# Mixer of a decoder trunk: all weight subtractions on VectorE, later differential products and merges, output tiles evacuated pair by pair

## The chip, the cores and the metric

The kernel runs on one core of one Trainium2 chip. The metric is the device time of one execution in microseconds (us). The engines are called PE (TensorE: matmuls), DVE (VectorE), ACT (ScalarE), POOL (GpSimd) and SP (SyncE, which issues the loads). Each of them works through its own list of instructions in the order in which the program holds them, and waits for the others by semaphores.

## What is computed

The program is a decoder trunk of two layers on 256 positions of width 1024. A layer is a half-step SwiGLU feed-forward block, a mixer, and a second feed-forward block; each has a normalization in front and a residual add behind it.

```python
for l in range(DEPTH):
    lam_init = 0.8 - 0.6 * math.exp(-0.3 * l)
    x = x + 0.5 * swiglu(rmsnorm(x, ffn1_norm[l]), ffn1_gate[l], ffn1_up[l], ffn1_down[l])
    x = x + mixer(rmsnorm(x, mix_norm[l]), cos, sin, w_in[l], w_out[l],
                  lambda_q1[l], lambda_k1[l], lambda_q2[l], lambda_k2[l],
                  subln_gain[l], dil_gain[l], lam_init)
    x = x + 0.5 * swiglu(rmsnorm(x, ffn2_norm[l]), ffn2_gate[l], ffn2_up[l], ffn2_down[l])
return rmsnorm(x, final_norm)
```

The mixer projects `h @ w_in` (3072 columns) into queries, keys and values of two attention families. The differential family has 4 heads with two score maps each: the weights are `a = softmax(s0) - lam * softmax(s1)` and the output is `a @ v`, normalized per head. The dilated family has 8 heads, whose three window patterns are merged into one mask here. Both outputs, side by side, are multiplied by `w_out`.

## The kernel before

All matmuls run in the 32-bit PE format with an error-compensated split. A weight tile of 128x1024 is loaded raw; ACT rounds it to a high part (`hi`, a CAST at L271, or at L267 for the columns of queries and keys), and a subtraction `raw - hi` gives the low part (`lo`, a TENSOR_TENSOR at the line behind, L272 or L267). The activations are split alike, as `xs` (high and low) at L328 and L333. PE then adds products of high and low parts. One such cast with its subtraction is a **tick**. Eight split tiles can be held ahead; a tick is skipped when none is free.

The feed-forward blocks are long runs of matmuls with ticks in between. The mixer is written as 112 **steps** of PE work. Steps 0 to 95 are the six column chunks of `w_in`, 16 steps each: queries and keys of the dilated family (chunks 0 and 1), of the differential one (2 and 3), then the values of the differential (4, steps 64 to 79) and dilated family (5, steps 80 to 95). A step of chunks 4 and 5 is three matmuls of 512 columns (L300 to L302). Steps 96 to 111 are the output projection: each multiplies four rows of 128 of `w_out` into one of eight output tiles (`wom`). Steps 96 to 99 and 103 to 106 finish output tiles 0 to 3; steps 100 to 102, 107 and 108 to 111 finish tiles 4 to 7.

What else has to be done is hung onto the steps by a table, `PLAN`: behind the matmuls of a step its jobs are issued, in the order of the text. Since every engine keeps the order of issue, the place of a job in the table decides what stands in front of it on its engine. The jobs that the change touches are these:

- `tick` (cast on ACT, subtraction on DVE) and `tick,p` (the same with the subtraction on POOL).
- `score` and `exp`: PE scores (L751), then for every head a masked minimum on DVE (`expos`, L767) and the exponential on ACT (L768), which also sums the denominators.
- `differ,t` for query block t: DVE inverts the denominators (`rd`, L777), scales (`cf`, L779), and combines the two maps of each head in place (four SCALAR_TENSOR_TENSOR on `exdif`, L782).
- `turnp`: PE transposes the weights (`trpdif`, L798) and ACT copies them out (`late`, L800).
- `value,4,t` and `value,5,t`: ACT scales the projected values (`vdif` L737, `vdil` L731). `vdif` of block 1 is written where the weights of block 0 stood, so it waits for the transposes of `turnp,dif,0,0`.
- `avdif` and `avdil` (PE, L806 and L829), `ndif` and `ndil` (normalization on ACT, DVE and POOL; the last operation of `ndif` is `mof` at L816), `merge` (PE transposes `trmdif` and `trmdil` at L844, then the split of the result on ACT and DVE).

The output tiles are evacuated by `chain` in pairs: DVE adds the first half of a tile to `x` (L880), ACT copies the second half (`half_w`, L377), DVE adds that (L882), ACT makes the high part of the next block's activations (L328), DVE the low part (L333), ACT the squares for the next norm (L338, L341). The first matmul of the next feed-forward block (`g_s`) writes into the PSUM buffer of output tile 4, so it waits for that tile's evacuation. Here `chain` is called once for tiles 0 to 3, behind step 106, and once for tiles 4 to 7, behind step 111.

Of the kernel before, what the change touches and what calls it, by code (L numbers as in the profile page):

```python
# [45 lines left out]
def _two_pi_parts():  # L46
# [20 lines left out]
    10: "norm",  # L67
    11: "tick tick",
    13: "tick",
    14: "tick,p",  # L70
    16: "table",
    17: "rope,0,0 rope,0,1",
    19: "tick",
# [2 lines left out]
    26: "tick",  # L76
    28: "tick",
    32: "rope,1,1",
    34: "tick",
    36: "score,dil,1 tick,p exp,dil,1,0 exp,dil,1,2 exp,dil,1,1 exp,dil,1,3",  # L80
    40: "rope,2,0",
    42: "turnp,dil,1,0 turnp,dil,1,1",
    43: "tick",
    46: "score,dil,0 tick,p exp,dil,0,0 exp,dil,0,2 exp,dil,0,1 exp,dil,0,3",
    47: "turnp,dil,1,2 turnp,dil,1,3",
    48: "rope,2,1",
    50: "tick",
# [3 lines left out]
    61: "tick",  # L91
    64: "rope,3,1",
    65: "tick",
    68: "score,dif,1 tick,p exp,dif,1,0 exp,dif,1,1 exp,dif,1,2 exp,dif,1,3",
    72: "value,4,0 differ,1",
    73: "tick",
    75: "score,dif,0 tick,p exp,dif,0,0 exp,dif,0,1 exp,dif,0,2 exp,dif,0,3",
    77: "turnp,dif,1,0",
    78: "differ,0",
    79: "turnp,dif,1,1",  # L100
    82: "value,4,1 tick",
    83: "turnp,dif,0,0",
    85: "avdif,0",
    86: "avdif,1 ndif,0",
    87: "tick ndif,1",
    88: "value,5,0",
    89: "merge,dif,0",
    90: "avdil,0,0 tick",
    92: "avdil,0,1 merge,dif,1",
    93: "ndil,0 tick",  # L110
    95: "value,5,1",
    96: "avdil,1,0 merge,dil,0",
    97: "avdil,1,1 ndil,1",
    98: "tick",
    99: "tick",
    100: "merge,dil,1",
# [2 lines left out]
    103: "tick",  # L119
    105: "tick",  # L120
    107: "tick",
    109: "tick",
}


# [1 line left out]
def trunk_kernel(ctx: ExitStack, tc: tile.TileContext, a: dict, out: bass.AP):  # L127
# [149 lines left out]
    def take(n):  # L277
        while len(split) < state["taken"] + n:
            for f in split_next():
                f()  # L280
        state["taken"] += n
        return split[state["taken"] - n:state["taken"]]

    def free(n):
        state["freed"] += n

    def tick(n, low="v"):

        got = []
        while len(got) < n and len(split) < min(state["freed"] + 8, total):  # L290
            got.append(split_next(low=low))
        return got

    def ticks(n, low="v"):
        for one in tick(n, low):
            for f in one:
                f()
# [64 lines left out]
    def mmw(ps, xs, wh, wl, start, stop, part="both"):  # L362

        def low():
            T.matmul(ps[:, :S], wl, xs[:, 0], start=False, stop=False)  # L365

        def high():
            T.matmul(ps, wh, xs.rearrange("p j s -> p (j s)"), start=start, stop=stop)  # L368
        if part != "both":
            (high if part == "high" else low)()  # L370
            return
        for f in ((high, low) if start else (low, high)):
            f()
# [33 lines left out]
    def chore(n):  # L407
        for _ in range(min(n, len(chores))):
            chores.pop(0)()
# [78 lines left out]
    def back(groups, src, nm, evac, nxt, order=None, beside=None):  # L488


        places = (acc, acc, acc, acc, scb, scb, trb, trb)
        w, accs = {}, {}
        for n, (hf, gi, d) in enumerate(order or [(h, g, d) for h in range(2) for g in range(len(groups)) for d in range(4)]):
            ks, last = groups[gi], gi == len(groups) - 1
            if d == 0:
                w[hf, gi] = take(len(ks) // 2)
            if gi == 0:
                accs[hf, d] = places[hf * 4 + d](f"{nm}{hf}{d}")
            for i, k in enumerate(ks):
                hi, lo = w[hf, gi][i // 2]  # L500
                c0 = (i % 2) * 512 + d * P
                mmw(accs[hf, d], src(k), hi[:, c0:c0 + P], lo[:, c0:c0 + P],
                    gi == 0 and i == 0, last and i == len(ks) - 1)
            if beside:
                beside(n)
            if d < 3:
                continue
            if not beside and not (last and hf):
                ticks(2)
            if last:  # L510
                chain([(hf * 4 + d, accs[hf, d]) for d in range(4)], evac, nxt)
            elif not beside:
                chore(5)
            free(len(ks) // 2)

    def chain(items, evac, nxt):

        prev = []
        for p in range(0, len(items), 2):
            pair = items[p:p + 2]  # L520
            evac(pair)
            for dt in prev:
                nxt.square(dt)
            prev = [dt for dt, _ in pair]
            for dt in prev:
                nxt.high(dt, x[:, dt])
            for dt in prev:
                nxt.low(dt, x[:, dt])
        for dt in prev:
            nxt.square(dt)  # L530

    def down(hs, nx, nm, nxt):
        def evac(pair):
            os = [half_of(ps, f"d{dt}_{nm}") for dt, ps in pair]
            for o, (dt, ps) in zip(os, pair):
                V.tensor_add(o, ps[:, :S], o)
            for o, (dt, ps) in zip(os, pair):
                V.scalar_tensor_tensor(o, o, 0.5, nx.row, op0=ALU.mult, op1=ALU.mult)
            for o, (dt, ps) in zip(os, pair):
                V.tensor_add(x[:, dt], x[:, dt], o)  # L540
        back([range(k, k + n) for k, n in DOWN], lambda k: hs[k], f"dn{nm}", evac, nxt)
# [114 lines left out]
    def mixer(l, nx, cs, consts, nxt):  # L656
# [220 lines left out]
        def evac(pair):  # L877
# [3 lines left out]
            for o, (dt, ps) in zip(os, pair):  # L881
                V.tensor_add(x[:, dt], x[:, dt], o)  # L882
        back((range(4), range(4, 8)), lambda k: mrg["dif" if k < 4 else "dil"][:, k % 4], f"wo{nm}", evac, nxt,
             OUT, lambda i: beside(len(STEPS) + i))

# [88 lines left out]
    for l in range(DEPTH):  # L974
        hs = up(nx, f"f{l}", "late" if l else "first", None if l else x_in, None if l else {2: rope_consts})
        nxt = Normed((2 + l) * KD, f"m{l}")
        down(hs, nx, f"f{l}", nxt)
        nx, nxt = nxt, Normed((4 + l) * KD, f"s{l}")
        mixer(l, nx, cs[0], consts, nxt)
        nx = nxt  # L980
        if l + 1 < DEPTH:
            hs = up(nx, f"s{l}", "late")
            nxt = Normed((l + 1) * KD, f"f{l + 1}")
# [49 lines left out]
```

## Time and profile before

| | us |
|---|---|
| median of three timed runs | 990.19 (990.14 to 990.96) |
| the profiled execution, its own time | 988.68 |
| its span, first to last instruction | 986.8 |
| PE busy in it | 974.4 (99%) |
| DVE busy | 704.2 (71%) |
| ACT busy | 556.9 (56%) |
| POOL busy | 67.9 (7%) |

The profile shows one execution. Times in its views are counted from the span's start. A row of a timeline gives start and duration in us, engine, line, operation, output<-inputs, and a count of merged instructions; in brackets stands the idle time of the engine ahead of it and what ended it. Matmuls overlap in the pipeline, so the pace of PE is read from one start to the next, not from the durations. The mixers lie at about 196 to 309 us (layer 0) and 680 to 793 us (layer 1).

### The profile page before, as it was taken

The numbers are of one execution on the slowest core, as the hardware profiler recorded it, in microseconds if no ns is written. First come the engines' busy times: TensorE is split into PE (matmuls) and PEld (weight loads), VectorE is DVE, ScalarE is ACT, GpSimd is POOL, SyncE is SP. The second block draws the span as 40 slices with busy tenths as digits, with TensorE's granted clock in tenths as the row PEclk, the third lists the DMA queues.
The fourth block names the chain that finished last, engine by engine and source line by source line (L and its number), as shares of the span: only waits on it lengthen the run. The fifth ranks groups of instructions, "written<-read, shape, count | busy, mean of one in ns | idle before, by whom it ended". The sixth has DMA issues, their size and how long they took to land.

```text
span 986.8 us, 15502 instructions
## 1 busy us (share of the span) xinstructions
PE 974.4 (99%) x5995; PEld 859.4 (87%) x5995; DVE 704.2 (71%) x1270; ACT 556.9 (56%) x994; POOL 67.9 (7%) x67
## 2 busy tenths in 40 slices
PE   8999999999999999999999999999999999999997
PEld 7888888899788888888888888889997888888886
DVE  6887788687668887775578777665876778687542
ACT  7765655356657665564357565454456566675432
POOL 0000000020212000000010000001112120000000
PEclk9999999999999999999999999999999999999999
DMA  9975565634435666565646665552652556656531
GB/s 293 274 217 173 181 198 178 210 129 141 159 100 168 213 214 192 172 204 202 214 140 193 186 206 194 194 211 90 210 169 88 172 161 185 203 177 184 200 129 44
DMA packets 134346, 176.80 MB, mean 179 GB/s; under 512 B 4944, under 2 KB 97280, under 8 KB 134272
## 3 DMA queue, kind: packets, MB, share of 16 engines
q1 hardware_dynamic: 134096, 175.54, 55.5%
q8 instruction: 47, 0.77, 0.3%
q10 hardware_dynamic: 176, 0.27, 0.1%
q14 instruction: 27, 0.22, 0.1%
HBM read 174.75 MB, written 1.05 MB: 178 GB/s over the span
## 4 chain that ended last, share of the span: by engine, by line
PE 93%; DVE 4%; ACT 1%; issue 1%; DMA 1%; SPq 0%; POOLq 0%; POOL 0%; ACTq 0%
PE g_s L368 8%; PE u_s L368 8%; PE dnf L368 8%; PE g_f L368 8%; PE u_f L368 8%; PE u_s L365 4%; PE u_f L365 4%; PE g_f L365 4%; PE g_s L365 4%; PE dnf L365 4%; PE dns L368 4%; PE pj_m L688 3%; PE pj_m L690 3%; PE pj_m L689 3%; PE dns L365 2%; PE dn_last L302 2%
## 5 line engine op out<-in xcount | busy, mean ns | idle before, releaser
L272 DVE TENSOR_TENSOR lo<-raw,hi 128x1024 fp32r<-128x1024 f32 (+1 forms) x293 | 352.8, 1223 | 138.9 <-ACT hi L271 138.1
L271 ACT CAST hi<-raw 128x1024 fp32r<-128x1024 f32 (+1 forms) x297 | 303.4, 1046 | 121.1 <-PE u_f L368 26.0
L368 PE MATMUL g_s<-xs_s,hi 128*128 128x512 f32 x352 | 127.3, 395 | 0.9 <-DVE x L880 0.9
L368 PE MATMUL u_s<-xs_s,hi 128*128 128x512 f32 x352 | 127.3, 395 | 0.0
L365 PE MATMUL u_s<-xs_s,lo 128*128 128x256 f32 x352 | 91.7, 281 | 0.0
L365 PE MATMUL g_s<-xs_s,lo 128*128 128x256 f32 x352 | 91.5, 280 | 0.0
L368 PEld LDWEIGHTS g_s<-xs_s,hi 128*128 128x128 f32 x352 | 66.0, 187 | 12.6 <-DVE x L880 1.5
L368 PEld LDWEIGHTS u_s<-xs_s,hi 128*128 128x128 f32 x352 | 66.0, 187 | 11.1
L688 PE MATMUL pj_m<-xs_m,hi 128*128 128x256 f32 x256 | 73.2, 286 | 0.0
L690 PE MATMUL pj_m<-xs_m,lo 128*128 128x256 f32 x256 | 71.8, 281 | 1.1 <-DVE lo L267 1.1
L689 PE MATMUL pj_m<-xs_m,hi 128*128 128x256 f32 x256 | 71.7, 280 | 0.0
L365 PEld LDWEIGHTS u_s<-xs_s,lo 128*128 128x128 f32 x352 | 66.5, 189 | 3.9
L365 PEld LDWEIGHTS g_s<-xs_s,lo 128*128 128x128 f32 x352 | 66.5, 189 | 3.7
L368 PE MATMUL g_f<-xs_in,hi 128*128 128x512 f32 x176 | 65.1, 401 | 0.0
L368 PE MATMUL u_f<-xs_in,hi 128*128 128x512 f32 x176 | 64.8, 400 | 0.0
L368 PE MATMUL u_f<-xs_f,hi 128*128 128x512 f32 x176 | 63.7, 395 | 0.0
L368 PE MATMUL g_f<-xs_f,hi 128*128 128x512 f32 x176 | 63.5, 394 | 0.0
L690 PEld LDWEIGHTS pj_m<-xs_m,lo 128*128 128x128 f32 x256 | 48.2, 188 | 1.3 <-DVE lo L267 1.3
L688 PEld LDWEIGHTS pj_m<-xs_m,hi 128*128 128x128 f32 x256 | 48.2, 188 | 1.0 <-issue 0.7
L689 PEld LDWEIGHTS pj_m<-xs_m,hi 128*128 128x128 f32 x256 | 48.2, 188 | 0.1
L267 DVE TENSOR_TENSOR lo<-raw,hi 128x1024 fp32r<-128x1024 f32 x28 | 36.0, 1320 | 14.6 <-ACT hi L267 14.6
L267 ACT CAST hi<-raw 128x1024 fp32r<-128x1024 f32 x32 | 31.6, 1048 | 25.6 <-DMA raw<-in_w_in_dram 8.9
(363 smaller groups left out, 2226.1 us busy)
## 6 DMA issues: line engine op xcount, KB each, us to landing
raw<-in_ffn_gate_dram SPq DMA_DIRECT2D x86, 512.0 KB, 4.0
raw<-in_ffn_up_dram SPq DMA_DIRECT2D x86, 512.0 KB, 5.1
raw<-in_ffn_down_dram SPq DMA_DIRECT2D x41, 1024.0 KB, 5.1
raw<-in_w_in_dram SPq DMA_DIRECT2D x24, 1024.0 KB, 5.2
raw<-in_w_out_dram SPq DMA_DIRECT2D x8, 1024.0 KB, 5.0
raw<-in_ffn_down_dram SPq DMA_DIRECT2D x6, 512.0 KB, 3.6
xt<-in_x_dram SPq DMA_DIRECT2D x3, 256.0 KB, 5.3
raw<-in_ffn_gate_dram SPq DMA_DIRECT2D x3, 256.0 KB, 5.5
```

The lines of the kernel that those rows point to most:

```text
L267: out = [lambda: A.copy(hi, raw), lambda: ENGINE[low].tensor_sub(lo, raw, hi.bitcast(F32))]
L271: out.append(lambda sl=sl: A.copy(hi[:, sl], raw[:, sl]))
L272: out.append(lambda sl=sl: ENGINE[low].tensor_sub(lo[:, sl], raw[:, sl], hi[:, sl].bitcast(F32)))
L302: T.matmul(ps, xl, wh, start=False, stop=stop)
L365: T.matmul(ps[:, :S], wl, xs[:, 0], start=False, stop=False)
L368: T.matmul(ps, wh, xs.rearrange("p j s -> p (j s)"), start=start, stop=stop)
L688: T.matmul(ps, hi, nx.xs[k][:, 0], start=k == 0, stop=False)
L689: T.matmul(ps, hi, nx.xs[k][:, 1], start=False, stop=False)
L690: T.matmul(ps, lo, nx.xs[k][:, 0], start=False, stop=k == KD - 1)
```

## The change

The table loses all `tick,p`; plain `tick` entries come at neighbouring steps. `avdif` goes from steps 85 and 86 to 86 and 87, the differential merges from 89 and 92 to 91 and 93, and the dilated products and norms move by up to four steps. In the last part `chain` is called for two tiles at a time, as soon as the second of them is finished: behind steps 104, 106, 109 and 111.

```diff
-    14: "tick,p",
...
-    34: "tick",
-    36: "score,dil,1 tick,p exp,dil,1,0 exp,dil,1,2 exp,dil,1,1 exp,dil,1,3",
+    33: "tick",
+    35: "tick",
+    36: "score,dil,1 exp,dil,1,0 exp,dil,1,2 exp,dil,1,1 exp,dil,1,3",
...
-    46: "score,dil,0 tick,p exp,dil,0,0 exp,dil,0,2 exp,dil,0,1 exp,dil,0,3",
+    45: "tick",
+    46: "score,dil,0 exp,dil,0,0 exp,dil,0,2 exp,dil,0,1 exp,dil,0,3",
...
-    68: "score,dif,1 tick,p exp,dif,1,0 exp,dif,1,1 exp,dif,1,2 exp,dif,1,3",
+    68: "score,dif,1 exp,dif,1,0 exp,dif,1,1 exp,dif,1,2 exp,dif,1,3",
+    70: "tick",
     72: "value,4,0 differ,1",
     73: "tick",
-    75: "score,dif,0 tick,p exp,dif,0,0 exp,dif,0,1 exp,dif,0,2 exp,dif,0,3",
+    75: "score,dif,0 exp,dif,0,0 exp,dif,0,1 exp,dif,0,2 exp,dif,0,3",
+    76: "tick",
     77: "turnp,dif,1,0",
     78: "differ,0",
     79: "turnp,dif,1,1",
-    82: "value,4,1 tick",
+    80: "value,4,1",
     83: "turnp,dif,0,0",
-    85: "avdif,0",
-    86: "avdif,1 ndif,0",
-    87: "tick ndif,1",
-    88: "value,5,0",
-    89: "merge,dif,0",
-    90: "avdil,0,0 tick",
-    92: "avdil,0,1 merge,dif,1",
-    93: "ndil,0 tick",
-    95: "value,5,1",
-    96: "avdil,1,0 merge,dil,0",
-    97: "avdil,1,1 ndil,1",
+    84: "tick",
+    86: "avdif,0",
+    87: "avdif,1 ndif,0",
+    88: "value,5,0 ndif,1",
+    89: "tick",
+    91: "merge,dif,0",
+    92: "tick",
+    93: "merge,dif,1",
+    94: "avdil,0,0 tick",
+    95: "value,5,1 avdil,0,1 ndil,0",
+    96: "avdil,1,0",
+    97: "avdil,1,1 ndil,1 merge,dil,0",
...
-    109: "tick",
+    108: "tick",
...
             if beside:
                 beside(n)
+            if beside and last and d % 2:
+                chain([(hf * 4 + e, accs[hf, e]) for e in (d - 1, d)], evac, nxt)
             if d < 3:
                 continue
-            if not beside and not (last and hf):
-                ticks(2)
-            if last:
-                chain([(hf * 4 + d, accs[hf, d]) for d in range(4)], evac, nxt)
-            elif not beside:
-                chore(5)
+            if not beside:
+                if not (last and hf):
+                    ticks(2)
+                if last:
+                    chain([(hf * 4 + e, accs[hf, e]) for e in range(4)], evac, nxt)
+                else:
+                    chore(5)
             free(len(ks) // 2)
```

What the tables make of it is seen in the order of the built programs. Line numbers of the changed kernel are 4 higher below the table and 7 higher below `back` (L271 is L275, L768 is L775). The order of loads on SP is the same in both. POOL has eight rows less, its four subtractions in each layer; the entry at step 14 issued nothing before, as no tile was free there.

On ACT, around the two blocks of differential exponentials of layer 0, there stood before (`hi` casts, exponentials of block 1 on 256 keys and of block 0 on 128 keys, copies of transposed weights and values):

```order
L271 CAST hi_2822<-raw_2787 128x1024
L768 ACTIVATE exdif_m_2826,den_m_2827<-exdif_m_2826,mxdif_m_2828 128x256 x2
...
L768 ACTIVATE exdif_m_2826,den_m_2827<-exdif_m_2826,mxdif_m_2843 128x256 x2
L737 ACTIVATE late_m_2861<-pj_m_2776,rs_m_2207 128x512
L271 CAST hi_2878<-raw_2876 128x1024
L271 CAST hi_2908<-raw_2876 128x1024
L768 ACTIVATE exdif_m_2912,den_m_2913<-exdif_m_2912,mxdif_m_2914 128x128 x2
...
L768 ACTIVATE exdif_m_2912,den_m_2913<-exdif_m_2912,mxdif_m_2929 128x128 x2
L800 COPY late_m_2861<-trpdif_m_2940 128x512
L800 COPY late_m_2861<-trpdif_m_2962 128x512
L737 ACTIVATE vdif_m_2978<-pj_m_2857,rs_m_2207 128x512
L271 CAST hi_2982<-raw_2980 128x1024
L800 COPY late_m_2861<-trpdif_m_2989 128x512
```

At the same place on ACT there stands now:

```order
L775 ACTIVATE exdif_m_2822,den_m_2823<-exdif_m_2822,mxdif_m_2839 128x256 x2
L275 CAST hi_2850<-raw_2787 128x1024
L744 ACTIVATE late_m_2861<-pj_m_2776,rs_m_2207 128x512
L275 CAST hi_2878<-raw_2876 128x1024
L775 ACTIVATE exdif_m_2908,den_m_2909<-exdif_m_2908,mxdif_m_2910 128x128 x2
...
L775 ACTIVATE exdif_m_2908,den_m_2909<-exdif_m_2908,mxdif_m_2925 128x128 x2
L275 CAST hi_2933<-raw_2876 128x1024
L807 COPY late_m_2861<-trpdif_m_2940 128x512
L807 COPY late_m_2861<-trpdif_m_2962 128x512
L744 ACTIVATE vdif_m_2972<-pj_m_2857,rs_m_2207 128x512
L807 COPY late_m_2861<-trpdif_m_2983 128x512
L275 CAST hi_2994<-raw_2992 128x1024
```

Each of the two casts has moved from ahead of a block of exponentials to behind it, and the cast between `vdif` and the last copy has moved behind that copy.

On DVE, from the last minimum of block 1 to the combination of block 0, there stood before (`lo` is a subtraction, `rd`, `cf`, `exdif`, `de` are `differ`):

```order
L767 ISA mxdif_m_2843 128x1
L777 RECIPROCAL rd_m_2863<-den_m_2827 128x4
L779 SCALAR_TENSOR_TENSOR cf_m_2865<-den_m_2827,lamn,rd_m_2863 128x4
L782 SCALAR_TENSOR_TENSOR exdif_m_2826<-exdif_m_2826,cf_m_2865 128x256 x4
L785 SCALAR_TENSOR_TENSOR de_m_2871<-den_m_2827 128x4
L272 TENSOR_TENSOR lo_2879<-raw_2876,hi_2878 128x1024
L767 ISA exdif_m_2912,mxdif_m_2914<-scdif_m_2888,mask_dif 128x128
...
L767 ISA mxdif_m_2929 128x1
L777 RECIPROCAL rd_m_2949<-den_m_2913 128x4
```

At the same place on DVE there stands now:

```order
L774 ISA mxdif_m_2839 128x1
L276 TENSOR_TENSOR lo_2851<-raw_2787,hi_2850 128x1024
L784 RECIPROCAL rd_m_2863<-den_m_2823 128x4
L786 SCALAR_TENSOR_TENSOR cf_m_2865<-den_m_2823,lamn,rd_m_2863 128x4
L789 SCALAR_TENSOR_TENSOR exdif_m_2822<-exdif_m_2822,cf_m_2865 128x256 x4
L792 SCALAR_TENSOR_TENSOR de_m_2871<-den_m_2823 128x4
L276 TENSOR_TENSOR lo_2879<-raw_2876,hi_2878 128x1024
L774 ISA exdif_m_2908,mxdif_m_2910<-scdif_m_2888,mask_dif 128x128
...
L774 ISA mxdif_m_2925 128x1
L276 TENSOR_TENSOR lo_2934<-raw_2876,hi_2933 128x1024
L784 RECIPROCAL rd_m_2949<-den_m_2909 128x4
```

A subtraction stands now between the minima of each block and its `rd`, where nothing stood.

On DVE, at the evacuation of output tiles 0 to 5, there stood before (`x<-wom` and `x<-x,half_w` are the two adds, `xs_s` the low parts):

```order
L272 TENSOR_TENSOR lo_3261<-raw_3257,hi_3260 128x1024
L272 TENSOR_TENSOR lo_3281<-raw_3257,hi_3280 128x1024
L880 TENSOR_TENSOR x<-wom_3119,x 128x256
...
L333 SCALAR_TENSOR_TENSOR xs_s_3302<-x,gains,xs_s_3302 128x256
L880 TENSOR_TENSOR x<-wom_3177,x 128x256
...
L333 SCALAR_TENSOR_TENSOR xs_s_3321<-x,gains,xs_s_3321 128x256
L272 TENSOR_TENSOR lo_3344<-raw_3340,hi_3343 128x1024
L272 TENSOR_TENSOR lo_3364<-raw_3340,hi_3363 128x1024
L880 TENSOR_TENSOR x<-wom_3205,x 128x256
```

At the same place on DVE there stands now:

```order
L276 TENSOR_TENSOR lo_3261<-raw_3257,hi_3260 128x1024
L887 TENSOR_TENSOR x<-wom_3119,x 128x256
...
L337 SCALAR_TENSOR_TENSOR xs_s_3282<-x,gains,xs_s_3282 128x256
L276 TENSOR_TENSOR lo_3300<-raw_3257,hi_3299 128x1024
L887 TENSOR_TENSOR x<-wom_3177,x 128x256
...
L337 SCALAR_TENSOR_TENSOR xs_s_3321<-x,gains,xs_s_3321 128x256
L276 TENSOR_TENSOR lo_3344<-raw_3340,hi_3343 128x1024
L276 TENSOR_TENSOR lo_3356<-raw_3340,hi_3355 128x1024
L887 TENSOR_TENSOR x<-wom_3205,x 128x256
```

The subtraction of step 105 has moved from ahead of the first pair to between the pairs; on ACT its cast now stands behind the squares of the first pair, and the copies of the second pair behind that cast.

## Rows read from the trace of the kernel before

**Rows 1.** The page, first part: busy time of PE, its share of the span and its instructions.

```profile
PE 974.4 (99%) x5995; PEld 859.4 (87%) x5995; DVE 704.2 (71%) x1270; ACT 556.9 (56%) x994; POOL 67.9 (7%) x67
```

**Rows 2.** Waits of PE in the stretch of the mixer of layer 0, 200 to 330 us (engine, output, line, what it waited for: us in total, times, longest).

```profile
PE pj_m L690 <- DVE lo L267: 1.1, 1, 1.1
PE avf_m L806 <- ACT late_m L800: 0.8, 1, 0.8
PE g_s L368 <- DVE x L880: 0.4, 1, 0.4
```

**Rows 3.** The same view for the mixer of layer 1, 684 to 790 us, and behind it the row of PE's timeline at the end of that mixer.

```profile
PE avf_m L806 <- ACT late_m L800: 0.9, 1, 0.9
...
792.87 0.51 PE L368 MATMUL g_s<-xs_s,hi 128*128 128x512 f32 x1 [0.45 <-DVE x L880]
```

**Rows 4.** Timeline of layer 0 around steps 33 to 36: DVE, POOL and PE.

```profile
217.16 4.56 DVE L267 TENSOR_TENSOR lo<-raw,hi 128x1024 fp32r<-128x1024 f32 x2
...
218.24 2.39 POOL L267 TENSOR_TENSOR lo<-raw,hi 128x1024 fp32r<-128x1024 f32 x1 [13.37 <-ACT hi L267]
...
220.42 0.28 PE L689 MATMUL pj_m<-xs_m,hi 128*128 128x256 f32 x1
221.77 0.39 PE L690 MATMUL pj_m<-xs_m,lo 128*128 128x256 f32 x1 [1.07 <-DVE lo L267]
```

**Rows 5.** Timeline of DVE in layer 0, the two `differ` and what lies between them.

```profile
258.42 0.18 DVE L777 RECIPROCAL rd_m<-den_m 128x4 f32<-128x4 f32 x1 [1.77 <-ACT exdif_m L768]
...
260.56 1.23 DVE L272 TENSOR_TENSOR lo<-raw,hi 128x1024 fp32r<-128x1024 f32 x1
261.69 0.29 DVE L767 CUSTOM_DVE_ANT_0 exdif_m<-scdif_m,mask_dif 128x128 f32<-128x128 f32 x1
...
265.31 0.18 DVE L777 RECIPROCAL rd_m<-den_m 128x4 f32<-128x4 f32 x1 [1.84 <-ACT exdif_m L768]
...
265.79 1.14 DVE L782 SCALAR_TENSOR_TENSOR exdif_m<-exdif_m,cf_m 128x128 f32<-128x128 f32 x4
```

**Rows 6.** Timeline of ACT in the same stretch: casts of steps 73 and 75, `vdif`, and the copy of the last transposes.

```profile
258.87 1.99 ACT L271 CAST hi<-raw 128x1024 fp32r<-128x1024 f32 x2
...
267.40 0.69 ACT L737 ACTIVATE vdif_m<-pj_m,rs_m 128x512 f32<-128x512 f32 x1 [1.17 <-PE trpdif_m L798]
...
268.93 0.59 ACT L800 COPY late_m<-trpdif_m 128x512 f32<-128x512 f32 x1
```

**Rows 7.** Timeline of PE in the same stretch: first and last transposes of the differential weights, matmuls of steps 84 and 85, `avdif,0`.

```profile
261.44 0.60 PE L798 MATMUL trpdif_m<-ident,exdif_m 128*128 128x128 f32 x4
...
266.50 0.80 PE L798 MATMUL trpdif_m<-ident,exdif_m 128*128 128x128 f32 x4
267.06 0.48 PE L300 MATMUL pj_m<-hi,xs_m 128*128 128x512 f32 x1
...
268.32 0.40 PE L302 MATMUL pj_m<-hi,xs_m 128*128 128x512 f32 x1
269.57 1.16 PE L806 MATMUL avf_m<-late_m 128*128 128x128 f32 x8 [0.84 <-ACT late_m L800]
```

**Rows 8.** Timeline of DVE in layer 0, the last operation of `ndif,0` and of `ndif,1`.

```profile
273.39 0.69 DVE L816 TENSOR_TENSOR mof_m<-avf_m,rsf_m 128x512 f32<-128x512 f32 x1 [1.12 <-POOL rsf_m L815]
...
277.14 0.69 DVE L816 TENSOR_TENSOR mof_m<-avf_m,rsf_m 128x512 f32<-128x512 f32 x1 [1.13 <-POOL rsf_m L815]
```

**Rows 9.** Timeline of layer 0 at the end of the output projection: PE (first matmul of step 105, last of step 111, first of the next block), DVE (first adds of pair 0, the subtractions of steps 107 and 109, first adds of the pair of tiles 4 and 5), ACT (high parts of pair 0, squares of the second pair, casts of steps 107 and 109).

```profile
298.96 0.28 PE L365 MATMUL wom<-mgdil_m,lo 128*128 128x256 f32 x1
...
308.45 0.40 PE L368 MATMUL wom<-mgdil_m,hi 128*128 128x512 f32 x1
309.29 0.50 PE L368 MATMUL g_s<-xs_s,hi 128*128 128x512 f32 x1 [0.44 <-DVE x L880]
...
299.70 0.75 DVE L880 TENSOR_TENSOR x<-wom,x 128x256 f32<-128x256 f32 x2
...
306.27 2.63 DVE L272 TENSOR_TENSOR lo<-raw,hi 128x1024 fp32r<-128x1024 f32 x2 [1.07 <-ACT hi L271]
308.82 0.74 DVE L880 TENSOR_TENSOR x<-wom,x 128x256 f32<-128x256 f32 x2
...
300.82 0.91 ACT L328 ACTIVATE xs_s<-x,gains 128x256 fp32r<-128x256 f32 x2 [1.29 <-DVE x L882]
...
304.58 0.71 ACT L341 ACTIVATE sq_s<-x 128x256 f32<-128x256 f32 x2
305.20 1.99 ACT L271 CAST hi<-raw 128x1024 fp32r<-128x1024 f32 x2
```

**Rows 10.** Timeline of PE in the kernel's first microseconds and its last matmul, and the view by windows for the last 2.8 us (columns: busy us and counts of PE, PEld, DVE, ACT, POOL, then granted TensorE clock, DMA share, GB/s).

```profile
5.41 0.77 PE L368 MATMUL g_f<-xs_in,hi 128*128 128x512 f32 x1
...
8.28 0.63 PE L368 MATMUL g_f<-xs_in,hi 128*128 128x512 f32 x1
8.71 0.63 PE L368 MATMUL u_f<-xs_in,hi 128*128 128x512 f32 x1
...
11.02 0.48 PE L365 MATMUL g_f<-xs_in,lo 128*128 128x256 f32 x2
...
980.32 0.28 PE L302 MATMUL dn_last<-hi,hE_s 128*128 128x256 f32 x1
...
984.00:986.80 2.80, 0.00 (x0) 0.00 (x0) 0.00 (x0) 0.00 (x0) 0.00 (x0) 0.50 0.49 182
```

## The prediction

> **What bounds the kernel now.** I read the busy times first: PE is busy for 974.4 of 986.8 us [rows 1], so a change on DVE, ACT or POOL can only show where PE waits for it. Next come the waits of PE in the two stretches that the change touches. In layer 0 there are three: 1.1 us for a subtraction, 0.8 us for a copy of transposed weights in front of `avf`, and 0.4 us for the evacuation add in front of `g_s` [rows 2]. Layer 1 has the last two only [rows 3]. That is all the change can win. What it can lose has to be read from the lists of DVE and ACT: wherever a moved cast or subtraction stands ahead of something that PE needs soon. Steps of chunks 4 and 5 follow each other at 0.234 us a matmul, 0.70 us a step (267.06 to 268.32 is five matmuls and a small start-up) [rows 7]. Times below are those of layer 0; layer 1 has the same lists.
>
> **Term A, subtractions off POOL: 1.2 us won, in layer 0 only.** While POOL's subtraction runs from 218.24 for 2.39 us, two DVE subtractions take 4.56 us together [rows 4]; two others without POOL's beside them take 2.63 us [rows 9] and a single one moves the next instruction on by 1.13 us (260.56 to 261.69) [rows 5]. So DVE lost about 2 us there, and PE stood from 220.42 to 221.77 instead of 0.12 us: 1.23 us. Without the POOL row the second subtraction ends near 219.5, a microsecond before PE wants it. The wait goes. In layer 1 no such wait is listed [rows 3], so nothing is won. The replacements cost DVE 1.13 us each. Those of steps 33, 35 and 45 stand ahead of the dilated minima, where DVE waits for PE's scores or has just got its 2 us back: I cost them at nothing; uncovered, each would be at most 1.13 us.
>
> **Term B, subtractions in front of `differ`: 4.2 us lost per layer.** Here the cover is missing. Before, the inversion of block 1 starts at 258.42, released by the last exponential, after 1.77 us of idle DVE; that of block 0 at 265.31, after 1.84 us [rows 5]. That idle time looks like room for a subtraction of 1.13 us. But its cast now stands on ACT behind all the exponentials of the block. So after the last exponential come a cast (1.99 us for two, so 0.95 to 1.04 for one) [rows 6], then the subtraction (1.13), and only then the inversion: 2.1 us later than before. This happens twice in a row, and the two add up, because the minima of block 0 stand on DVE behind the `differ` of block 1. Inversion 1 moves from 258.42 to 260.5, the minima of block 0 from 261.69 to 263.8, its exponentials with them, and inversion 0 from 265.31 to 269.5. The combination at 265.79 moves to 270.0.
>
> PE is not that patient. The first transposes (261.44) have some room: inversion and two combinations end near 261.9, which costs 0.3 to 0.4 us. The last ones (266.50) have none: already before, four transposes took 0.56 us up to the next matmul (267.06), where other transposes of four take 0.35, since each waits for its head's combination [rows 7]. So PE reaches the matmul at 267.06 as much later as the combinations: 4.2 us, the first wait included. It will stand some 3.5 us in one piece.
>
> **Term C, the copy before `avdif,0`: 1.0 us won per layer.** Before, `vdif` starts at 267.40, after the transposes, then comes a cast, then the copy at 268.93 [rows 6]; `avf` starts at 269.57, though PE could have at 268.32 + 0.23 = 268.55 [rows 7]. Now the copy stands right behind `vdif` and `avdif,0` a step later. With the transposes ending near 271.26, `vdif` starts 0.34 us later and the copy is done 0.69 + 0.59 us after that, at 272.9; PE arrives after three steps, at 273.4. The wait of 1.02 us is gone, with half a microsecond to spare. Terms B and C leave 3.2 us per layer.
>
> **Moved merges and dilated products: nothing.** The last operation of `ndif,0` ended 4.5 us after the start of `avf` (269.57 to 274.08) [rows 7, 8], so now near 277.9; the merge stands behind step 91, which PE reaches near 279.7 (0.9 us for `avdif,0`, 1.7 for `avdif,1`, five steps). `ndif,1` ends near 280.6 with the second merge at 281.6: about 1 us of room. What PE does in this stretch is the same work in another order. If a cover fails, what is late is at most some tenths; I keep 0.5 us per layer for the upper end.
>
> **Term D, evacuation pair by pair: 1.1 us lost per layer.** PE has done output tile 1 at 298.96, yet DVE begins with pair 0 at 299.70, since four subtractions stand ahead of it [rows 9]. Now three do, so the second add of the pair can start as soon as tile 1 can be read, near 299.2. That is the gain meant. Then the pair runs through: from the second add (300.03 before) the high parts come 0.8 us later, and with two squares of 0.71 us together behind them ACT is through 2.35 us after that add, near 301.5. But the cast of step 105 now stands here (to 302.5), its subtraction waits for it (to 303.7), and the second pair starts behind the subtraction. Its squares end 2.7 us later, near 306.4. Behind them stand the casts of two ticks, which began at 305.20 before; `g_s` came 4.09 us after that, at 309.29. So `g_s` comes near 310.4. PE is through its last matmul at 308.45 + 0.23 = 308.68: a wait of 0.6 us becomes 1.7. Adds and copies that were far apart are not faster for being split; a cast on ACT, with its subtraction, is now inside the chain that sets the end. The bounds are 0.6 us won (the wait vanishes) and 1.6 us lost.
>
> **Sum.** Per layer 4.2 - 1.0 + 1.1 = 4.3 us lost; twice that, less 1.2 in layer 0, is 7.3 us. The profiled execution took 988.68 us (span 986.8 and 1.9 around it), which makes 996.0. The median of the timed runs lies 1.5 us above it, so 990.19 + 7.3 = **997.5 us**. The measurement tells 0.2%, 2.0 us, from no change.
>
> **Rivals.** (1) *The tail gains.* Terms A to C hold, but tile 4 is free in time, since the split lets the first pair go early and ACT's squares overlap. Then both waits of 0.6 us go instead of growing: 990.19 + 2 x (3.2 - 0.6) - 1.2 = 994.2. Against it stands the place of the cast and subtraction between the pairs. (2) *The clock falls.* In the last 2.8 us of the kernel the granted clock was 0.50, the level of 1.2 GHz, with PE's last matmul started at 980.32 [rows 10]; so some microseconds without work lower it, and term B makes a gap of 3.5 us where none was above 1.3. At the low level 512 columns take 0.43 us (8.28 to 8.71) [rows 10] instead of 0.234, so each slow microsecond costs half of itself. At the start such a stretch lasted at most from 5.41 to 11.02 [rows 10], so 0 to 2.8 us per gap, 1.4 in the middle: 997.5 + 2.8 = 1000.3. The Trainium skill, "TensorE: Matmul & The Clock Gate", section "Why this matters for your kernels", warns of gaps between bursts of matmuls for this reason: they send the clock back to the half level. By that rule the change would land at this rival's time; no wait within the trace of before is long enough to show it. (3) *Faster.* If the casts reach ACT early enough for the subtractions to fall wholly into the idle 1.77 and 1.84 us ahead of the inversions, term B is nothing, and A, C and the vanished waits of the tail remain: 990.19 - 1.2 - 2 x 1.0 - 2 x 0.6 = 985.8. It decides at a cast that ends 1.13 us before the last exponential; the order on ACT puts it a microsecond behind it. (4) *Nothing to tell:* the gaps of term B are made good by shorter waits later. There are hardly any later waits to shorten [rows 2, 3]. That the change doesn't do what it says is excluded by the order: POOL has no subtraction left.
>
> **How the numbers follow.** Forecast 0.55 (997.5), tail gains 0.13 (994.2), clock falls 0.22 (1000.3), faster 0.07 (985.8), nothing to tell 0.03. The range takes in the first three: from 994.2 less half a microsecond of rounding, 993.7, to the forecast with term D at 1.6, failing covers of 0.5 per layer and most of a clock loss: 997.5 + 1.0 + 1.0 + 2.0 = 1001.5. That leaves out the two last cases and a long slow stretch, under 2 in 10. Slower by over 0.2%: 0.90; within: 0.03; faster: 0.07.
>
> **What would show it.** Right: a new PE wait for DVE `exdif` at the last differential transposes, over 3 us in each layer; the inversions idle only until a subtraction that itself waits for ACT's cast; no PE wait for `late` and none for a projection's `lo`; a wait of 1 to 2 us in front of `g_s`. The granted clock there says whether rival 2 holds. Wrong: no wait at those transposes, which would mean that the cast ran ahead of the exponentials; or `g_s` without a wait, which is rival 1.

## The result: 1001.9 us instead of 990.6, and the profile after

| | before | after |
|---|---|---|
| median of four timed runs, us | 990.58 (990.14 to 991.08) | 1001.91 (1001.0 to 1002.88) |
| profiled execution, own time | 988.68 | 1002.53 |
| its span | 986.8 | 1000.7 |
| mean granted clock of PE | 0.998 | 0.990 |

The changed kernel is slower by 11.3 us: the ratio is 1.0117, 95% interval 1.0105 to 1.013. The time lies 0.4 us above the upper end of the forecast range; the kernel before, timed anew, came out 0.4 us above the 990.19 from which the forecast started.

The page's first row, as in [rows 1]:

```profile
PE 980.8 (98%) x5995; PEld 864.7 (86%) x5995; DVE 705.5 (71%) x1278; ACT 556.3 (56%) x994; POOL 45.7 (5%) x59
```

PE has the same 5995 instructions and is busy 6.4 us longer. While it waits it is not busy, so some matmuls must have run more slowly. The waits of PE over the whole span (columns as in [rows 2]) show the rest:

```profile
PE trpdif_m L805 <- DVE exdif_m L789: 6.9, 2, 3.4
PE g_s L372 <- DVE x L887: 3.6, 2, 1.8
```

The waits of [rows 2, 3] for `lo` and `late` are gone. The one ahead of `g_s` has grown from 0.4 to 1.8 us in each layer, and there is a new one of 3.4 us at the last differential transposes. Their cause stands on DVE, timeline of layer 0, the same stretch as [rows 5]:

```profile
258.08 1.23 DVE L276 TENSOR_TENSOR lo<-raw,hi 128x1024 fp32r<-128x1024 f32 x1 [2.70 <-ACT hi L275]
259.22 0.17 DVE L784 RECIPROCAL rd_m<-den_m 128x4 f32<-128x4 f32 x1
...
262.49 0.28 DVE L774 CUSTOM_DVE_ANT_0 exdif_m<-scdif_m,mask_dif 128x128 f32<-128x128 f32 x1
...
267.04 1.23 DVE L276 TENSOR_TENSOR lo<-raw,hi 128x1024 fp32r<-128x1024 f32 x1 [2.78 <-ACT hi L275]
268.18 0.17 DVE L784 RECIPROCAL rd_m<-den_m 128x4 f32<-128x4 f32 x1
...
268.64 1.14 DVE L789 SCALAR_TENSOR_TENSOR exdif_m<-exdif_m,cf_m 128x128 f32<-128x128 f32 x4
```

The brackets show it: DVE stands for 2.70 and 2.78 us ahead of the two subtractions, last of all for their casts on ACT, and the inversion starts the moment the subtraction is through. PE in the same stretch, as in [rows 7]:

```profile
265.31 0.40 PE L306 MATMUL pj_m<-hi,xs_m 128*128 128x512 f32 x1
269.14 1.02 PE L805 MATMUL trpdif_m<-ident,exdif_m 128*128 128x128 f32 x4 [3.44 <-DVE exdif_m L789]
269.92 0.47 PE L304 MATMUL pj_m<-hi,xs_m 128*128 128x512 f32 x1
...
271.02 0.63 PE L304 MATMUL pj_m<-hi,xs_m 128*128 128x512 f32 x1
271.45 0.63 PE L305 MATMUL pj_m<-lo,xs_m 128*128 128x512 f32 x1
...
273.58 1.12 PE L813 MATMUL avf_m<-late_m 128*128 128x128 f32 x8
```

The reader should look at the starts behind the wait: 271.02 to 271.45 is 0.43 us a matmul of 512 columns, where it was 0.234. The windows over the two gaps of layer 0 (columns as in [rows 10], the third from the end is the granted clock):

```profile
269.00:270.00 1.00, 0.86 (x5) 0.58 (x5) 0.85 (x4) 0.00 (x0) 0.00 (x0) 1.00 0.54 31
270.00:271.00 1.00, 1.00 (x4) 0.80 (x4) 0.00 (x0) 0.74 (x2) 0.00 (x0) 0.65 0.88 340
271.00:272.00 1.00, 1.00 (x4) 0.78 (x3) 0.00 (x0) 1.00 (x2) 0.00 (x0) 0.50 1.04 406
272.00:273.00 1.00, 1.00 (x4) 0.81 (x3) 0.59 (x1) 0.37 (x1) 0.00 (x0) 0.50 0.71 272
273.00:274.00 1.00, 1.00 (x6) 0.81 (x6) 0.63 (x1) 0.00 (x0) 0.00 (x0) 0.64 0.00 0
274.00:275.00 1.00, 1.00 (x9) 0.92 (x8) 0.00 (x0) 0.26 (x1) 0.00 (x0) 1.00 0.00 0
...
314.00:315.00 1.00, 1.00 (x6) 0.88 (x7) 0.87 (x3) 0.43 (x2) 0.00 (x0) 0.84 0.57 33
315.00:316.00 1.00, 1.00 (x4) 0.85 (x4) 0.88 (x2) 1.00 (x5) 0.07 (x1) 0.50 0.68 190
...
317.00:318.00 1.00, 1.00 (x5) 0.81 (x5) 1.00 (x3) 0.22 (x1) 0.46 (x1) 0.50 1.08 375
318.00:319.00 1.00, 1.00 (x7) 0.91 (x6) 0.76 (x3) 1.00 (x4) 0.00 (x0) 0.96 0.23 72
```

After both gaps PE resumes at full clock, and about a microsecond later the clock is granted at 0.50 (1.2 GHz) for about three microseconds. In layer 1 the same happens behind `g_s`. Behind its transposes, where PE resumes at 759.90, the clock has fallen while PE still stood, and it is back at 765.2 only:

```profile
758.00:759.00 1.00, 0.00 (x0) 0.00 (x0) 1.00 (x2) 0.73 (x2) 0.00 (x0) 0.70 0.00 0
759.00:760.00 1.00, 0.10 (x1) 0.13 (x1) 0.93 (x6) 0.00 (x0) 0.00 (x0) 0.50 0.00 0
...
764.00:765.00 1.00, 1.00 (x5) 0.81 (x4) 0.54 (x1) 0.00 (x0) 0.00 (x0) 0.50 0.00 0
765.00:766.00 1.00, 1.00 (x9) 1.00 (x9) 0.00 (x0) 0.00 (x0) 0.00 (x0) 0.88 0.00 0
```

The end of the output projection, as in [rows 9]: PE, then DVE, and below it the adds of the second pair before the change.

```profile
311.74 0.40 PE L372 MATMUL wom<-mgdil_m,hi 128*128 128x512 f32 x1
313.93 0.50 PE L372 MATMUL g_s<-xs_s,hi 128*128 128x512 f32 x1 [1.80 <-DVE x L887]
```

```profile
306.14 1.23 DVE L276 TENSOR_TENSOR lo<-raw,hi 128x1024 fp32r<-128x1024 f32 x1 [1.08 <-ACT hi L275]
307.28 0.75 DVE L887 TENSOR_TENSOR x<-wom,x 128x256 f32<-128x256 f32 x2
...
310.89 2.65 DVE L276 TENSOR_TENSOR lo<-raw,hi 128x1024 fp32r<-128x1024 f32 x2 [1.06 <-ACT hi L275]
313.46 0.74 DVE L887 TENSOR_TENSOR x<-wom,x 128x256 f32<-128x256 f32 x2
```

```profile
302.17 0.75 DVE L880 TENSOR_TENSOR x<-wom,x 128x256 f32<-128x256 f32 x2
```

The subtraction between the pairs waits 1.08 us for its cast and moves the next instruction on by 1.14. The adds of the second pair start 5.1 us later than before (302.17, now 307.28), and those of tiles 4 and 5 4.6 us later (308.82 [rows 9], now 313.46), where PE's last matmul is 3.3 us later.

**Where the 13.9 us between the two spans lie**, read from the shift of the same matmul in both traces. Start of the last `pj` ahead of the first differential transposes: 261.21, now 259.93, -1.28. `pj` behind the last transposes: [rows 7] 267.06, now 269.92, +2.86. `avf`: 269.57 plus the step that it was moved by (0.70), now 273.58, +3.31. Last matmul of step 111: [rows 9] 308.45, now 311.74, +3.29. `g_s`: 309.29, now 313.93, +4.64. Behind the slow stretch there (`ssp_s`, 316.38, now 322.56): +6.18. Layer 1 repeats it: last `pj` ahead of the first transposes 744.81, now 750.70, +5.89; behind the last transposes 750.68, now 760.73, +10.05; `avf` 753.18 plus 0.70, now 764.72, +10.84; last matmul of step 111 792.03, now 803.05, +11.02; `g_s` 792.87 [rows 3], now 805.23, +12.36; `ssp_s` 799.97, now 813.88, +13.91.

### The profile page after: what moved, and what is told of

Read it like the earlier page. It is cut to its first block, busy times and chain, and to the rows that moved or that the text cites. A ratio compares the mean times of both kernels' runs of the same rounds, so it can differ in the third digit from the quotient of the medians.

```text
span 1000.7 us, 15499 instructions
## 1 busy us (share of the span) xinstructions
PE 980.8 (98%) x5995; PEld 864.7 (86%) x5995; DVE 705.5 (71%) x1278; ACT 556.3 (56%) x994; POOL 45.7 (5%) x59
## 4 chain that ended last, share of the span: by engine, by line
PE 92%; ACT 3%; DVE 3%; issue 1%; DMA 0%; SPq 0%; POOLq 0%; POOL 0%; ACTq 0%
PE g_s L372 8%; PE u_s L372 8%; PE u_f L372 8%; PE g_f L372 8%; PE dnf L372 8%; PE u_s L369 4%; PE g_s L369 4%; PE u_f L369 4%; PE g_f L369 4%; PE dnf L369 4%; PE dns L372 4%; PE pj_m L695 3%; PE pj_m L697 3%; PE pj_m L696 3%; PE dns L369 2%; PE dn_last L306 2%
## 5 line engine op out<-in xcount | busy, mean ns | idle before, releaser
L276 DVE TENSOR_TENSOR lo<-raw,hi 128x1024 fp32r<-128x1024 f32 (+1 forms) x297 | 357.6, 1222 | 152.9 <-ACT hi L275 149.8
L275 ACT CAST hi<-raw 128x1024 fp32r<-128x1024 f32 (+1 forms) x297 | 303.9, 1046 | 121.0 <-PE u_f L372 25.8
L372 PEld LDWEIGHTS u_s<-xs_s,hi 128*128 128x128 f32 x352 | 67.1, 191 | 11.3
L271 DVE TENSOR_TENSOR lo<-raw,hi 128x1024 fp32r<-128x1024 f32 x32 | 38.3, 1236 | 14.6 <-ACT hi L271 14.6
L369 PE MATMUL u_f<-xs_f,lo 128*128 128x256 f32 x176 | 45.8, 281 | 0.0
```

The lines of the kernel that those rows point to most:

```text
L271: out = [lambda: A.copy(hi, raw), lambda: ENGINE[low].tensor_sub(lo, raw, hi.bitcast(F32))]
L275: out.append(lambda sl=sl: A.copy(hi[:, sl], raw[:, sl]))
L276: out.append(lambda sl=sl: ENGINE[low].tensor_sub(lo[:, sl], raw[:, sl], hi[:, sl].bitcast(F32)))
```

## Experiments

Each kernel was timed next to the kernel before. Its median there was 990.6 for both subtractions moved, for four tiles at once (with and without them moved) and for the pairs alone; 989.8 for the fillers and for the parts in the kernel before; 990.0 for the rest. Ratios and the distances that are compared are to that median: the changed kernel stands 11.3 us above its own.

**Both subtractions out of the way.** The ticks in front of the inversions are issued earlier and later:

```diff
     65: "tick",
+    67: "tick",
...
-    70: "tick",
...
-    76: "tick",
     77: "turnp,dif,1,0",
-    78: "differ,0",
+    78: "differ,0 tick",
```

> The changed kernel with its tick of step 70 at step 67 (cast and subtraction ahead of the exponentials of block 1) and its tick of step 76 at step 78, behind differ,0. Theory (the loss comes from a cast and a subtraction standing in front of each inversion, and from the clock falling behind the gap): PE's wait at the last differential transposes goes from 3.4 us to under 0.4 in both layers, the granted clock stays at 1.00 there, the wait at g_s stays near 1.8; the time falls from 1001.9 to about 992.6 (990 to 994). Rival (load: VectorE simply has four more subtractions per layer and PE waits for it wherever they stand): the wait only changes its place, the time stays above 999.

Measured: 989.95 us (989.43 to 992.12), ratio 0.9995 (0.9986 to 1.0005). No wait at the transposes is left, so VectorE's load is not what PE waits for. The time is 2.6 us under the one expected, just below its range. It stands 0.7 us below the kernel before, so these two entries cost 12.0 us. Of that 2 x 4.1 is lost ahead of the transposes; the other 3.8 is what is left for the clock behind the two waits. The next two move one of them at a time (one half of the diff each).

> Changed kernel with only the cast and subtraction of step 70 issued at step 67, ahead of the exponentials of block 1; the subtraction in front of the inversion of block 0 stays. Theory (each of the two subtractions puts 2.1 us into the wait at the last transposes, and they add up): that wait becomes 1.2 to 1.5 us instead of 3.4 in both layers, and the time falls by 2 x 2.0 to 997.9 as far as the work goes. What the clock does behind a gap of that length is open: if it stays, as in the kernel before, where the longest gap was 1.07 us, another 2 x 1.6 go and the time is 994.5; if it falls, 997.9. Rival (they overlap, the later one alone makes the wait): the wait stays over 3 us and the time within 1 us of 1001.9.

> Changed kernel with only the cast and subtraction of step 76 issued behind the combination of block 0; the subtraction in front of the inversion of block 1 stays. Theory: the same 2.1 us go from the wait at the last transposes, which becomes 1.2 to 1.5 us; the wait at the first transposes (some tenths) stays. Time 994.5 if the clock stays up behind such a gap, 997.9 if it falls. The two kernels of this pair should lie within 1.5 us of each other. Rival (the first subtraction is hidden by idle DVE time and costs nothing): this kernel lies at 990, like the one with both moved, and its sister at 1001.

Measured: 995.95 us (994.89 to 997.97) and 993.68 us (991.52 to 995.17). PE of the first, the last transposes in layers 0 and 1, and below it the second, layer 0:

```profile
267.50 1.03 PE L805 MATMUL trpdif_m<-ident,exdif_m 128*128 128x128 f32 x4 [1.68 <-DVE exdif_m L789]
...
756.23 1.02 PE L805 MATMUL trpdif_m<-ident,exdif_m 128*128 128x128 f32 x4 [1.68 <-DVE exdif_m L789]
```

```profile
267.54 1.02 PE L804 MATMUL trpdif_m<-ident,exdif_m 128*128 128x128 f32 x4 [1.37 <-DVE exdif_m L788]
```

Neither is hidden: moving one takes 1.8 or 2.1 us off the wait of 3.4, moving both all of it. Both rivals fall. The two lie 2.3 us apart, further than forecast. The waits differ by 2 x 0.3 us; the clock may account for the rest, since in the profiled executions it fell behind three of the first kernel's four gaps and one of the second's.

**Four tiles at once again** (the rest as changed; the tick of step 108 goes back to 109):

```diff
-            if beside and last and d % 2:
-                chain([(hf * 4 + e, accs[hf, e]) for e in (d - 1, d)], evac, nxt)
...
+            if last:
+                chain([(hf * 4 + d, accs[hf, d]) for d in range(4)], evac, nxt)
```

> The changed kernel with the evacuation of four tiles at once and the last tick at step 109, as before the change. Theory (the tick between the two pairs is what makes g_s late, and its gap lowers the clock too): the wait at g_s falls from 1.8 to about 0.4 us, the clock stays at 1.00 behind it, the wait at the transposes stays at 3.4; the time falls from 1001.9 to about 998.5 (997 to 999.5). Rival (the pairwise evacuation wins, as the split is meant to; the g_s wait comes from the stretch being later as a whole): no change or slower, 1001.5 to 1003.

Measured: 996.89 us (996.66 to 997.87), ratio 1.0065 (1.005 to 1.008), 6.3 above the kernel before, so 5.0 less than the changed kernel. Its waits of PE:

```profile
PE trpdif_m L802 <- DVE exdif_m L786: 6.9, 2, 3.4
...
PE g_s L372 <- DVE x L884: 0.9, 2, 0.4
```

The clock stays at 1.00 behind `g_s` and falls behind the transposes only. Of the 5.0 us, 2 x 1.35 is waiting, which leaves 2.3 for the clock. The reverse puts the pairs alone into the kernel before.

> The kernel before with the pairwise evacuation alone, and its last tick at step 108. Theory: g_s waits about 1.8 us in each layer instead of 0.4, and the clock falls behind it; 990.6 + 2 x 1.35 + 0 to 3.1 is 993.3 to 996.4. Rival (splitting wins once the stretch is not late): the wait at g_s goes, 989.4.

Measured: 995.69 us (994.98 to 995.9), ratio 1.005 (1.0035 to 1.0065). The wait ahead of `g_s` is 1.8 us in both layers, and the clock fell in layer 0 but not in layer 1 of the profiled execution.

**Is it the split or the tick inside it?** The kernel with both subtractions moved keeps the pairs, and its tick of step 105 is issued at 104, ahead of the first pair:

```diff
-    105: "tick",
+    104: "tick",
```

> Kernel with both subtractions moved (989.95), tiles still evacuated pair by pair, but the cast and subtraction of step 105 issued at step 104, ahead of pair 0 instead of between the pairs. Theory (the tick between the pairs costs, not the split): the squares of pair 1 end about 1.7 us earlier, the wait in front of the first matmul of the next block falls from 1.8 us to 0.1 to 0.5, the clock stays up behind it, and the time is 989.95 - 2 x 1.5 - (0 to 3) = 984 to 987. Rival (splitting the four tiles into pairs costs by itself): that wait stays over 1.2 us and the time is 989 to 991.

Measured: 985.38 us (984.73 to 986.13), ratio 0.9953 (0.9941 to 0.9966): 4.6 us below the kernel before, where the tick between the pairs left 0.7. The wait ahead of `g_s` in it:

```profile
PE g_s L371 <- DVE x L886: 0.9, 2, 0.4
```

So it is the tick between the pairs that costs, 3.9 us, 2 x 1.35 of it as waiting, and not the split. But the split wins nothing either: with both subtractions moved and four tiles at once the wait is the same, and so is the time but for 0.2 us.

> Both edits together: the ticks of steps 70 and 76 moved to 67 and 78, and four tiles evacuated at once. What is left of the change is the subtractions off GpSimd and the later products and merges. Theory: only its gains are left, no PE wait over 0.5 us in the mixers; 990.6 less 1.2 to 2.4 (subtractions off GpSimd) less 2.0 (copy before avdif,0) is about 986.8 (985.5 to 988). Rival (load): slower than before, above 991.

Measured: 985.57 us (984.97 to 986.36), ratio 0.995 (0.9935 to 0.9964). A last try at the 0.4 us, on this kernel:

```diff
-    107: "tick",
-    109: "tick",
+    106: "tick tick",
```

> Kernel with both subtractions moved and four tiles evacuated at once (985.57), with the ticks of steps 107 and 109 issued at step 106, ahead of the evacuation of tiles 0 to 3 instead of between the two evacuations. Theory: the evacuation of tiles 4 to 7 finds DVE and ACT free when PE has finished tile 4, so the wait of 0.4 us in front of the next block goes to nothing in both layers: 984.7 (984.2 to 985.3). Rival (the first evacuation moves back by as much as the second gains, since the casts and subtractions are only moved): the wait stays at 0.3 to 0.6 us and the time at 985.6, or over 986 if later low parts of the next block come late.

Measured: 985.77 us (985.41 to 987.11). Nothing was won, but not in the rival's way: DVE has no subtraction any more between the two evacuations. The two ticks were skipped, as no tile was free at step 106, and the next block started two split tiles short. The wait of 0.4 us is gone, and PE waits for subtractions instead, 0.31 and 0.17 us in each layer:

```profile
312.65 0.39 PE L367 MATMUL g_s<-xs_s,lo 128*128 128x256 f32 x1 [0.31 <-DVE lo L274]
313.78 0.39 PE L367 MATMUL g_s<-xs_s,lo 128*128 128x256 f32 x1 [0.17 <-DVE lo L274]
```

**The clock by itself.** If the slow matmuls make up what the waits don't explain, then filling the gaps of the changed kernel with useless work, while everything behind them starts when it did, must win back just that. Matmuls with a weight tile of zeros add nothing to tiles that are being summed up:

```diff
-    83: "turnp,dif,0,0",
+    83: "fill,14 turnp,dif,0,0",
...
+        def fill(n):
+            for _ in range(n):
+                T.matmul(pjs[5, 0], zr, w[0][0][:, :512], start=False, stop=False)
```

> The changed kernel with 14 matmuls of 512 columns by a zero weight tile, added into the running accumulation of step 83 ahead of the last differential transposes, so that PE works through its gap there (3.3 us of work in a gap of 3.4). Theory (part of the loss is the clock, which falls because PE stands still): the transposes start when they did, the matmuls behind them keep 0.234 us instead of 0.43, the granted clock stays at 1.00 there; the time falls by 3 to 4 us, to about 998.4, by doing more work. Rival (the slow matmuls have another cause, such as the loads that land there at 340 to 406 GB/s): they stay at 0.43 and the time stays at 1001.9 or rises.

> As the run with the first gap filled, and 8 more such matmuls behind step 110 into output tile 7, so that PE works through the gap in front of g_s too (1.9 us of work). Theory: the clock holds there as well; a further 2 to 3 us less, about 995.3. Rival: no further change, or later by the work added.

Measured: 997.92 us (996.18 to 998.63) with the gaps at the transposes filled, and 996.65 us (996.08 to 997.18) with eight such matmuls also behind step 110. That is 8.2 and 6.9 us above the kernel before instead of 11.3: with 28 and 44 matmuls more the kernel is 3.1 and 4.4 us faster. Of the second, PE at the fillers in layer 0, and the windows over the stretches that ran at 0.50:

```profile
309.47 0.40 PE L375 MATMUL wom<-mgdil_m,hi 128*128 128x512 f32 x1
309.71 2.02 PE L874 MATMUL wom<-mgdif_m,zr 128*128 128x512 f32 x8
```

```profile
269.00:275.00 6.00, 5.83 (x33) 4.56 (x32) 3.18 (x9) 3.14 (x5) 0.00 (x0) 1.00 0.54 178
314.00:320.00 6.00, 6.00 (x37) 5.27 (x36) 3.48 (x8) 4.82 (x12) 2.96 (x4) 1.00 0.53 173
```

In layer 0 the transposes start 3.84 us behind the start of the last `pj` (265.97 to 269.81, with the fillers in between), as against 3.83 in the changed kernel: the delay itself has stayed. The clock is 1.00 throughout, with the same loads: 178 GB/s in the first stretch, where the changed kernel's six rows average 175. So the loads don't make the matmuls slow. The second filler won 1.3 us, less than the 2 to 3 expected. What is left, 6.9 us (ratio 1.0069, 1.0053 to 1.0086), is the change without the clock, close to the 7.3 of the forecast's sum.

**The other parts alone, in the kernel before.** First every `tick,p` made a `tick` where it stands, the four of a layer alike:

```diff
-    75: "score,dif,0 tick,p exp,dif,0,0 exp,dif,0,1 exp,dif,0,2 exp,dif,0,3",
+    75: "score,dif,0 tick exp,dif,0,0 exp,dif,0,1 exp,dif,0,2 exp,dif,0,3",
```

> The kernel before with every tick,p made a plain tick at its own step: the subtractions move from GpSimd to VectorE and nothing else does; the casts stay ahead of the exponentials. Theory: the wait of 1.2 us for lo goes (in layer 0 of the profile, in some executions in both layers), and only block 0 gets later, by one subtraction of 1.1 us per layer: 990.6 - 1.2 to 2.4 + 2.2 is 990.4 to 991.6, no inversion waits for a cast. Rival (load): the four subtractions cost their full 1.13 us each, 8 of them, 998 or more.

Measured: 990.52 us (989.64 to 991.53), ratio 1.0008 (0.9998 to 1.0017). The wait for `lo` goes, and a new one comes, of 0.7 us in each layer:

```profile
PE trpdif_m L798 <- ACT late_m L800: 1.5, 2, 0.7
```

There the subtractions stand ahead of the exponentials, with their casts, and cost little: what costs is their place behind the exponentials, not that VectorE does them. Second, only the table's entries of steps 80 to 97 as in the diff of the change:

> The kernel before with the table entries of steps 80 to 97 of the changed one alone (values, differential products, merges, dilated products and their ticks). Theory: the wait for the copy before avdif,0 goes, nothing else moves: 990.6 - 2.0 is 988.6. Rival (the later merges push the end of the mixer): slower than 990.6, with a new wait at the merges or at g_s.

Measured: 986.87 us (985.33 to 988.8), ratio 0.9973 (0.9964 to 0.9982). The wait for `late` is gone, the rest of [rows 2] stays. It gained 2.9 us, where the wait explains 2.0; the other 0.9 is not explained, and the runs spread over 3.5 us.

## Why the prediction was right about the work and wrong about the time

**Term A: right.** No wait for `lo` is left in layer 0. The two subtractions of [rows 4] that took 4.56 us beside POOL's now take 2.35 (DVE, changed kernel):

```profile
217.24 2.35 DVE L271 TENSOR_TENSOR lo<-raw,hi 128x1024 fp32r<-128x1024 f32 x2
```

The term was 1.2 us, and PE reaches the first transposes of layer 0 1.28 us earlier than before.

**Term B: right.** Forecast 4.2 us per layer; from ahead of the first transposes to behind the last the shift grows by 4.1 in layer 0 (-1.28 to +2.86) and 4.2 in layer 1 (+5.89 to +10.05). The two subtractions add up as the prediction had it, one at a time showing 1.8 and 2.1 us. Rival 3, that the casts come early enough, is refuted by the 2.70 and 2.78 us of idle DVE that end with the casts.

**Term C: right.** No wait for `late` is left, with slow matmuls or (both subtractions moved) without, and the part alone is faster.

**Moved merges: right.** From `avf` to the last matmul of step 111 the shift stays at +3.3 us in layer 0; in layer 1 it grows by 0.2, in the `avf` matmuls that still run at half clock.

**Term D: right, a little small.** 1.1 forecast, 1.35 in layer 0 and 1.34 in layer 1. The wait ahead of `g_s` is 1.8 us where 1.7 was forecast; rival 1, that the tail gains, is refuted as long as the tick stands between the pairs.

**The step that failed is the clock, which the sum put at nothing and left to rival 2, and its price there.** The terms that the sum has come to -1.28 + 4.1 + 4.2 + 2 x (1.35 - 1.02) = 7.7 us, against 7.3; the spans differ by 13.9. The rest is the clock: read from the starts, 1.5 us behind the transposes and 1.5 behind `g_s` in layer 0, 1.8 and 1.5 in layer 1, 6.3 together (0.3 won between the mixers and 0.2 lost in `avf` nearly cancel). The forecast gave the falling clock 0.22, though it had the row for it (the half level at the end [rows 10]) and a gap of 3.5 us of its own making. And it priced the fall for the two gaps of term B alone, at 1.4 each, which was near the mark for those. It left out the waits ahead of `g_s`, which its own term D put at 1.7 us; the trace of before had no row for gaps between 1.1 us and several. There lay the clock's other 3 us, and the time above the range. The Trainium skill, "TensorE: Matmul & The Clock Gate", section "Why this matters for your kernels", warns that gaps between bursts of matmuls send the clock back to the half level. The trace agrees for the two gaps of 3.44 us. The gaps of 1.78 and 1.80 us are shorter than those that the Trainium skill warns of there, and behind them the granted clock was 0.50 too; there the measurement decides.

**What stays open.** The medians differ by 11.3 us, the profiled spans by 13.9. The profiled execution of before was 1.9 us faster than its median and that of after 0.6 slower. The clock's share differs from one execution to the next: of the changed kernel's four runs two had a mean granted clock of 0.990 (1002.53 and 1002.88 us) and two of 0.992 (1001.3 and 1001.0). In the profiled execution of the kernel with the pairs alone, the wait for `lo` stands in both layers, not in layer 0 alone; that the timed runs of the kernel before often had it twice would explain over a microsecond, but no row of those runs shows it. The whole change with its faults undone (both subtractions moved, four tiles at once) won 5.1 us and the later products alone 2.9; the 2.2 between them is also nearer to two such waits than to one.

## What to carry to other kernels

Idle time of an engine ahead of a step on the path is room for more work only if that work's own input is there in time: read where the input stands in its producer's list before the gap is called free. In this kernel a gap on PE of 1.7 us or more cost its length and then, more often than not, 1.5 to 1.8 us in slow matmuls, so a list that makes such a gap is to be priced with both. When several changes come together, undo them one at a time: here the later products alone were worth 2.9 us, and all of the change with its three badly placed subtractions moved is 4.6 us faster than before.

## What the runs showed of the hardware that had not been expected

The clock fell behind gaps much shorter than the several microseconds at the end of the kernel before, and not each time. Counted over the profiled executions of all kernels here, both mixers, by PE's wait and the granted clock in the six microseconds behind it:

| wait of PE, us | what for | fell to 0.50 |
|---|---|---|
| 3.43 to 3.44 | last transposes | 4 of 4 |
| 1.78 to 1.80 | `g_s` | 9 of 12 |
| 1.68 | last transposes, first moved | 1 of 2 |
| 1.37 | last transposes, second moved | 0 of 2 |
| 0.2 to 1.1 | `lo`, `late`, `g_s`, transposes | 0 of 32 |

Where it fell, PE ran at full clock again first, for 0.15 to 1.4 us, except behind the 3.44 us of the changed kernel in layer 1, where the clock had fallen before PE resumed. The same kernel can fall or not: with the second subtraction moved, the wait ahead of `g_s` was 1.79 us in layer 0 and 1.80 in layer 1, and the clock fell in the first alone.
